# Where a layer input's projection lies: behind the end of the first projection, or beside the cached attention

## The chip, the cores and the metric

One NeuronCore of a Trainium2 chip runs the whole program. It has TensorE (PE: matrix products and transposes, with its weight loads shown apart as PEld), VectorE (DVE), ScalarE (ACT), GpSimd (POOL), and SyncE (SP), whose queue issues all of this kernel's transfers in order. The metric is the device time of one execution in microseconds (us); lower is better.

## The reference

One layer of a streaming encoder, over a prompt of 1024 tokens and 8 decode rows of 16 tokens with a cached past of 1024 (DEPTH is 1, D_MODEL 1024). Cut to what matters here:

```python
h = rmsnorm(x, g_mix)
q_a, k_a, v_a, q_b, k_b, v_b = split_heads(h, w_in)      # two groups of 8 heads x 64
a = stick_breaking(q_a, k_a, v_a, q_pos, k_pos)          # group A: sigmoid, running product over keys
o_b = chunk_band_prompt(q_b, k_b, v_b, rel_table)        # group B: softmax over 9 chunks of 64, with a bias
mix = jnp.concatenate([rmsnorm(a), rmsnorm(o_b)], axis=-1)
x = x + mix @ w_out
h = rmsnorm(x, g_ffn)
x = x + (silu(h @ w_gate) * (h @ w_up)) @ w_down
gate = sigmoid(rmsnorm(x, g_ple) @ w_ple_gate)
x = x + gate * (p @ w_ple_proj)                          # p: the layer input, 256 wide
```

The last line's `p @ w_ple_proj` depends on nothing else: it may be computed at any time, is stored to HBM, and is read again at the kernel's end. It is the work that the change moves.

## The kernel before

All products are of float32 accuracy: an operand is split in a high part (a cast on ScalarE, `whi`, `hTh`, `wth`, `pTh`) and the rest (a subtraction, `wlo`, `hTl`, `wtl`, `pTl`), and three products are summed (`mm3`, lines 100 to 102). Weights pass through the class `Chunks`: `raw` loads one chunk (`wraw`, one buffer), `parts` splits it into one of two places (`pair`), casting on ScalarE (line 159) and subtracting on GpSimd (line 105). So a third chunk can be split only when the products of the first have been read, and a new chunk loaded only when the last one is split.

The work is written as generators, and a few helpers interleave them: `advance(main, side, ratio, steps)` takes steps of `main` and `ratio` steps of `side` after each, and `along(a, b, ratio, due)` makes one sequence of two. Their numbers set the order in which work is handed to a scheduler, which then orders each engine's queue by its own estimate of when operands are ready. The engines run their queues strictly in that order.

In order of time:
- `qkv`: the first projection, in chunks of `w_in`, the last of them being queries of group B; first beside the cached attention of group A, then beside the prompt's attention, 1.95 units of it per step. It ends near 510 us.
- `attention`: 128 units, one for a head and a tile of 128 queries; eight units make a head, the first eight heads are group A. A unit's scores go to a bank `S` (two banks), for group A through two sigmoids on ScalarE (`w` and `keep`, lines 582 and 583), a running product on VectorE (`between`: `TENSOR_TENSOR_SCAN`, lines 111 and 114) and a product on GpSimd (line 592). Five units later `flip` transposes the weights (line 610) and splits them (`wth`, `wtl`); `outputs` multiplies with the values (`po`, lines 633 and 634), `turn` transposes a head's result (`ob`, line 648). In group B there is a bias and a minimum on VectorE (line 586) and an exponential on ScalarE (line 594). Sigmoid and exponential need different tables: at a switch ScalarE has an `ACT_TABLE_LOAD`.
- behind the projection: the cached attention of group B (`decode(1, ...)`: transposes of the cache `draw`, scores `sdec`, results `acc`) and `embed`, the layer input's projection, beside 43 units of attention. `embed` asks for its weights at its first step; SP issues that transfer far ahead, in the projection, but their split comes behind the product on GpSimd of the last group-A unit (`tc.issue_after(kept[-1].ins)`). Then, for each of nine token tiles, `turned` loads the layer input (`pn`, line 833), transposes and splits it (`pT`), and two steps of six products each (`pj`) follow, in the same banks `S`; ScalarE copies them out (`pjo`, line 853).
- `half_out`, beside the rest of attention: `mix` fetches finished heads (`mixn`, lines 894 and 898), transposes them (line 904) and casts them (`hUh`, line 907); then products with the first half of `w_out` (`acc`). Where attention has ended, the other heads' `mixn` follow, and the second half (`lower`, line 1001).
- the feed-forward part, the gate and the final norm, from some 820 us on.

Of the kernel before, what the change touches and what calls it, by code (L numbers as in the profile page):

```python
# [17 lines left out]
ALU = mybir.AluOpType  # L18
# [4 lines left out]
P = 128  # L23
D = 1024
# [15 lines left out]
def tile_hymba_step(  # L40
# [38 lines left out]
    V, A, G, T = nc.vector, nc.scalar, nc.gpsimd, nc.tensor  # L79
# [19 lines left out]
    def mm3(out, ah, al, bh, bl, start, stop):  # L99
        T.matmul(out, lhsT=ah, rhs=bh, start=start, stop=False)  # L100
        T.matmul(out, lhsT=ah, rhs=bl, start=False, stop=False)  # L101
        T.matmul(out, lhsT=al, rhs=bh, start=False, stop=stop)  # L102

    def sub(eng, out, a, hi):
        return eng.tensor_tensor(out, a, hi.bitcast(F32), op=ALU.subtract)  # L105

    def between(keep, own):

        n, d = keep.shape[1], own.shape[1]
        rev = keep[:, n - d :][:, ::-1]  # L110
        V.tensor_tensor_scan(rev, rev, own[:, ::-1], 0.0, op0=ALU.mult, op1=ALU.max)
        if n > d:
            rev = keep[:, : n - d][:, ::-1]
            V.tensor_tensor_scan(rev, rev, zero[:, 0:1].to_broadcast([P, n - d]), keep[:, n - d : n - d + 1], op0=ALU.mult,  # L114
                                 op1=ALU.max)
# [50 lines left out]
    def cols(w, c, n=256):  # L166
        return w[:, c * n : (c + 1) * n].rearrange("(k p) c -> p k c", p=P)
# [59 lines left out]
    def qkv(ch, hT, stg, first, second):  # L227
# [75 lines left out]
        def load(i, cuts=2):  # L303
            if i < len(loads):
                grp, w, c = loads[i]
                ready[loads[i]] = ch.load(cols(w_in[0], (grp * 3 + w) * 2 + c), KT, 256, cuts)

        ready[loads[0]] = first
        for i, (grp, w, c) in enumerate(loads):
# [200 lines left out]
            yield  # L510


    kept = []

    def attention(ap_, ps, lag):
        def prepare(p8):
# [30 lines left out]
        def bias(st, hh):  # L547
            if st["pr"] or hh:
                toep = ap_.tile([P, (8 - hh * 2) * P], F32, name="toep", tag=f"keep{1 + hh}")[:, :640]
            else:  # L550

                toep = ps["early"].tile([P, 640], F32, name="toep", tag="toep", bufs=1)
            nc.sync.dma_start(toep, rel[st["pr"] * 2 + hh])
            if st["pr"] or hh:
                G.tensor_scalar(toep, toep, -1.0, None, op0=ALU.mult)
            else:
                A.activation(toep, toep, AF.Copy, scale=-1.0)
            G.memset(toep[0:64, 576:640], -NEG)
            G.memset(toep[64:128, 0:64], -NEG)
            st[hh]["toep"] = toep  # L560

        def scores(st, hh, t):
            grp, hd = st["grp"], st[hh]
            if grp and "toep" not in hd:
                bias(st, hh)
            kb0 = max(0, t - 4) if grp else 0
            n = (t + 1 - kb0) * P
            w = ap_.tile([P, (t + 1) * P], F32, name="w", tag=f"wa{t}")[:, :n]
            if not grp:
                keep = ap_.tile([P, (7, 8, 6)[t % 3] * P], F32, name="keep", tag=f"keep{t % 3}")[:, :n]  # L570
            cut = {5: 384, 6: 512, 7: 512, 8: 512}.get(n // P, n)
            qs = slice(t * P, (t + 1) * P)
            mx = None
            for lo, hi in ((0, cut), (cut, n)):
                if lo == hi:
                    break
                sc = ps["s"].tile([P, 512], F32, name="S", tag="S")[:, : hi - lo]
                kc = slice(kb0 * P + lo, kb0 * P + hi)
                T.matmul(sc, lhsT=hd["qq"][:, qs], rhs=hd["kkh"][:, kc], start=True, stop=False)  # L579
                T.matmul(sc, lhsT=hd["qq"][:, qs], rhs=hd["kkl"][:, kc], start=False, stop=True)  # L580
                if not grp:
                    A.activation(w[:, lo:hi], sc, AF.Sigmoid)
                    A.activation(keep[:, lo:hi], sc, AF.Sigmoid, scale=-1.0)  # L583
                else:
                    m = ap_.tile([P, 1], F32, name="mxp", tag="mxp", bufs=6)
                    V.tensor_tensor_reduce(w[:, lo:hi], sc, hd["toep"][:, 640 - n + lo : 640 - n + hi], 1.0,
                                           3e38 if mx is None else mx, ALU.add, ALU.min, accum_out=m)
                    mx = m
            if not grp:
                between(keep, ident)  # L590
                G.memset(w[:, n - 1 :], 0.0)
                kept.append(G.tensor_tensor(w[:, : n - 1], w[:, : n - 1], keep[:, 1:], op=ALU.mult))  # L592
            else:
                A.activation(w, w, AF.Exp, bias=mx, scale=-1.0, accum_out=st["rs"][:, hh, t : t + 1])
            return w
# [125 lines left out]
    def pool(stack, name, side, bufs=1):  # L721
        return stack.enter_context(tc.tile_pool(name=name, bufs=bufs, side=side, reuse_waits="tile"))
# [10 lines left out]
    def advance(main, side, ratio, steps=None):  # L733

        due, n = 0.0, 0
        while steps is None or n < steps:
            if next(main, "end") == "end":
                break
            n += 1
            due += ratio  # L740
            while due >= 1.0:
                due -= 1.0
                next(side, None)
        return n

    ch = Chunks(pool(ctx, "w1", "left"), "w", 2048, 1, 2)
# [10 lines left out]
    with tc.tile_pool(name="x1", bufs=2, side="right") as xp, tc.manual_schedule(engines=all_engines):  # L757
# [26 lines left out]
        transposed(ps["t"], rows.pop(0), hT, 0)  # L784
        rows += [row(1), row(2)]
        project = qkv(ch, hT, stg, w_first, ch.raw(cols(w_in[0], 3), KT, 256))
        next(project)
        transposed(ps["t"], rows.pop(0), hT, 1)
# [16 lines left out]
    dec = decode(0, Chunks(dp, "d", 1024, RAWS, 2), dp)  # L805
# [11 lines left out]
    att = run(range(8))  # L817
# [6 lines left out]
    dec = decode(1, Chunks(dp, "d", 1024, RAWS - 1, 2), dp)  # L824
    pp = ps["early"] = pool(dstack, "pp", "right", 2)

    def embed():

        with tc.issue_after(kept[-1].ins):
            wj = ch.load(w_ple_proj[0].rearrange("(k p) c -> p k c", p=P), 2, D)  # L830
        def turned(t):
            pn = pp.tile([P, 256], F32, name="pn", tag="pn")
            nc.sync.dma_start(pn, p_tok[t])
            pt = ps["t"].tile([P, 512], F32, name="pt", tag="T")
            for j in range(2):
                T.transpose(pt[:, j * P : (j + 1) * P], pn[:, j * P : (j + 1) * P], ident)
            pT = [pp.tile([P, 2, P], F32R, name=f"pT{n}", tag=f"pT{n}", bufs=PT) for n in "hl"]
            pv = pt[:, :256].rearrange("p (k n) -> p k n", k=2)
            A.copy(pT[0], pv)
            sub(V, pT[1], pv, pT[0])  # L840
            return pT

        nxt = turned(0)
        yield
        for t in range(NT):
            pT = nxt
            for c in range(2):
                cs = slice(c * 512, c * 512 + 512)
                ps_ = ps["s"].tile([P, 512], F32, name="pj", tag="S")
                for k in range(2):  # L850
                    mm3(ps_, pT[0][:, k], pT[1][:, k], wj[0][:, k, cs], wj[1][:, k, cs], k == 0, k == 1)
                o = pp.tile([P, 512], F32, name="pjo", tag="pjo", bufs=2)
                A.copy(o, ps_)
                nc.sync.dma_start(proj[t * P : (t + 1) * P, cs], o)
                if c == 0 and t + 1 < NT:
                    nxt = turned(t + 1)
                yield
# [5 lines left out]
    def along(a, b, ratio, due):  # L863

        for _ in a:
            yield
            due += ratio
            while due >= 1.0:
                due -= 1.0
                if next(b, "end") != "end":  # L870
                    yield
        yield from b

    next(dec)
    advance(att, dec, 0, 3)
    beside = along(dec, embed(), 1.2, -3.0)
    advance(att, beside, 1.0, 40)
    for _ in beside:
        pass
    dstack.close()  # L880
# [85 lines left out]
    def bank(n=512):  # L966
        return ps_o.tile([P, 512], F32, name="ps", tag="O")[:, :n]
# [15 lines left out]
    def gate_up_parts(v, eng=None):  # L983
        return ch.parts(v, KT, 256, 4, eng)
# [101 lines left out]
    def sum_parts(i, v, eng=G):  # L1086
        out = [p4.tile([P, 4, P], F32R, name=f"S{i}{n}", tag=f"S{i}{n}", bufs=1) for n in "hl"]
        marks[:] = A.copy(out[0], v[i]), sub(eng, out[1], v[i], out[0])
        return out
# [7 lines left out]
    with ExitStack() as planned:  # L1097
        for i in range(NT + SKEW):
# [14 lines left out]
            if j == NT - 2:  # L1113
                w = gate_up_parts(raw, V)
# [15 lines left out]
    with tc.tile_pool(name="ph4b", bufs=2, side="right", reuse_waits="tile") as p4b:  # L1130
# [12 lines left out]
        for i in range(n_chunk):  # L1143
# [25 lines left out]
            c = bank()  # L1169
# [37 lines left out]
            if more:  # L1207
                S, w = {**S_next, 3: sum_parts(3, s)}, nxt
# [401 lines left out]
    for p in range(4):  # L1610
# [14 lines left out]
        c = bank()  # L1625
# [90 lines left out]
```

## Time and profile before

| | us |
|---|---|
| median of 3 runs | 1716.88 |
| lowest and highest | 1714.91, 1718.3 |
| the profiled execution | 1712.64 |
| its span, in which the rows below lie | 1710.6 |
| mean granted TensorE clock in the span | 0.99 |

A row of a timeline gives start, length, engine, line, operation, what it writes and reads, and in brackets how long its engine stood idle before it and what ended that. A row of the chain of waits gives start, length and what. In a table by stretch each engine has its busy time and the number of its instructions; PEclk is the share of full clock that TensorE was granted. Matmuls are pipelined: the start of the next says more of one's cost than its own length.

### The profile page before, as it was taken

The page shows a single profiled execution, that of the slowest core. Times are in us where ns is not written, and L with a number is a line of the kernel's source. Part 1 is how long each engine was busy: PE and PEld are TensorE (multiplying, and loading weights), DVE is VectorE, ACT ScalarE, POOL GpSimd, SP SyncE. Part 2 cuts the span into 40 slices and gives each one's busy share as a digit, 9 for nine tenths or more (in the row PEclk, how much of TensorE's full clock was granted, in tenths as well). Part 3 has the DMA queues.
Part 4 walks back from the last instruction along what each step waited for, and adds up shares of the span by engine and source line. Part 5 has one row for each costly group of instructions (what it writes and reads, how often), then busy time and mean ns, then how long its engine had stood idle before and what let it go on. Part 6 is the DMA issues. An engine that isn't in the chain of part 4 may idle for free.

```text
span 1710.6 us, 27738 instructions
## 1 busy us (share of the span) xinstructions
PE 1651.7 (97%) x10308; PEld 1421.3 (83%) x10308; DVE 1099.0 (64%) x1716; ACT 807.1 (47%) x1713; POOL 805.7 (47%) x652
## 2 busy tenths in 40 slices
PE   8999999989997999898989999999999999999998
PEld 7999888989996887787868888888888878878887
DVE  6111444379889666854787666666565597798875
ACT  5323545366778777643543233333332244433673
POOL 2313301277356411322345555555555379968763
PEclk9999999999998999999999999999999999999999
DMA  5847888665369885854422222222222597722222
GB/s 193 276 151 219 275 292 293 187 187 168 116 181 277 276 266 163 252 176 169 153 82 96 96 96 95 96 93 87 86 89 95 214 367 256 257 79 111 99 98 99
DMA packets 172810, 293.49 MB, mean 172 GB/s; under 512 B 16642, under 2 KB 96258, under 8 KB 170371
## 3 DMA queue, kind: packets, MB, share of 16 engines
q1 hardware_dynamic: 172674, 291.71, 52.0%
q8 instruction: 82, 1.34, 0.3%
q14 instruction: 54, 0.43, 0.1%
HBM read 204.77 MB, written 86.90 MB: 171 GB/s over the span
## 4 chain that ended last, share of the span: by engine, by line
PE 78%; DVE 7%; DMA 6%; ACT 3%; POOL 3%; issue 2%; SPq 1%; POOLq 0%; DVEq 0%; ACTq 0%
PE ps L1058 24%; PE ps L100 6%; PE ps L101 6%; PE ps L102 6%; PE pt L1321 4%; PE pt L1058 3%; PE ps L1321 3%; PE pt L610 2%; PE pt L405 2%; PE acc L468 2%; DMA v<-sv 2%; DVE keep L114 2%; PE po L634 1%; PE sdec L427 1%; PE S L579 1%
## 5 line engine op out<-in xcount | busy, mean ns | idle before, releaser
L105 POOL TENSOR_TENSOR wlo<-wraw,whi 128x512 fp32r<-128x512 f32 (+1 forms) x119 | 211.3, 1798 | 139.7 <-ACT whi L159 138.5
L100 PE MATMUL ps<-whi,hTh 128*128 128x256 f32 x576 | 167.7, 291 | 1.3 <-ACT st L267 1.3
L101 PE MATMUL ps<-wlo,hTh 128*128 128x256 f32 x576 | 164.2, 285 | 0.0
L102 PE MATMUL ps<-whi,hTl 128*128 128x256 f32 x576 | 163.7, 284 | 0.1
L159 ACT CAST whi<-wraw 128x512 fp32r<-128x512 f32 (+1 forms) x122 | 88.6, 744 | 71.4 <-PE ps L1058 28.6
L100 PEld LDWEIGHTS ps<-whi,hTh 128*128 128x128 f32 x576 | 110.4, 192 | 7.9 <-issue 5.7
L592 POOL TENSOR_TENSOR w<-w,keep 128x127 f32<-128x127 f32 (+4 forms) x64 | 78.6, 1230 | 74.8 <-DVE keep L114 64.5
L102 PEld LDWEIGHTS ps<-whi,hTl 128*128 128x128 f32 x576 | 110.4, 192 | 0.8 <-DVE hTl L105 0.4
L101 PEld LDWEIGHTS ps<-wlo,hTh 128*128 128x128 f32 x576 | 110.5, 192 | 0.2
L614 ACT CAST wth<-pt 128x512 fp32r<-128x512 f32 (+1 forms) x192 | 84.4, 466 | 44.5 <-PE pt L610 43.9
L105 DVE TENSOR_TENSOR wtl<-pt,wth 128x512 fp32r<-128x512 f32 (+1 forms) x192 | 94.1, 513 | 14.8 <-ACT wth L614 14.7
L114 DVE TENSOR_TENSOR_SCAN keep<-keep,zero 128x128 f32<-128x128 f32 (+7 forms) x64 | 101.6, 1588 | 1.7
L610 PE MATMUL pt<-ident,w 128*128 128x128 f32 x528 | 90.4, 284 | 8.5 <-DVE wtl L105 4.4
L610 PEld LDWEIGHTS pt<-ident,w 128*128 128x128 f32 x528 | 64.2, 144 | 21.6 <-DVE wtl L105 6.0
L579 PE MATMUL S<-qk 128*128 128x384 f32 (+2 forms) x192 | 71.9, 376 | 6.5 <-ACT keep L583 4.4
L633 PE MATMUL po<-wth,vk 128*128 128x256 f32 (+1 forms) x304 | 76.5, 283 | 1.5 <-DVE wtl L105 1.2
L105 POOL TENSOR_TENSOR actl<-actr,acth 128x1024 fp32r<-128x1024 f32 (+1 forms) x22 | 61.2, 2782 | 34.2 <-DMA sr<-acts 20.7
L634 PE MATMUL po<-wtl,vk 128*128 128x256 f32 (+1 forms) x304 | 73.4, 285 | 0.0
L406 DVE COPY kT<-pt 128x512 f32<-128x512 f32 x48 | 33.0, 687 | 53.4 <-PE pt L405 49.5
L101 PE MATMUL ps<-hTl,whi 128*128 128x384 f32 x192 | 65.4, 341 | 0.0
L102 PE MATMUL ps<-hTh,wlo 128*128 128x384 f32 x192 | 65.3, 340 | 0.0
L100 PE MATMUL ps<-hTh,whi 128*128 128x384 f32 x192 | 65.3, 340 | 0.0
(441 smaller groups left out, 5292.1 us busy)
## 6 DMA issues: line engine op xcount, KB each, us to landing
draw<-in_cache_sb_k SPq DMA_DIRECT2D x32, 512.0 KB, 5.7
draw<-in_cache_sb_v SPq DMA_DIRECT2D x32, 512.0 KB, 5.7
act<-sg SPq DMA_DIRECT2D x11, 1152.0 KB
actr<-act SPq DMA_DIRECT2D x22, 576.0 KB, 9.5
wraw<-in_w_in SPq DMA_DIRECT2D x11, 1024.0 KB, 8.7
wraw<-in_w_gate SPq DMA_DIRECT2D x11, 1024.0 KB, 5.5
wraw<-in_w_up SPq DMA_DIRECT2D x11, 1024.0 KB, 5.4
v<-sv SPq DMA_DIRECT2D x36, 256.0 KB, 4.7
```

The costliest lines, as they stand in the source:

```text
L100: T.matmul(out, lhsT=ah, rhs=bh, start=start, stop=False)
L101: T.matmul(out, lhsT=ah, rhs=bl, start=False, stop=False)
L102: T.matmul(out, lhsT=al, rhs=bh, start=False, stop=stop)
L105: return eng.tensor_tensor(out, a, hi.bitcast(F32), op=ALU.subtract)
L114: V.tensor_tensor_scan(rev, rev, zero[:, 0:1].to_broadcast([P, n - d]), keep[:, n - d : n - d + 1], op0=ALU.mult, op1=ALU.max)
L159: A.copy(h[:, o], v[:, o])
L579: T.matmul(sc, lhsT=hd["qq"][:, qs], rhs=hd["kkh"][:, kc], start=True, stop=False)
L610: T.transpose(pt[:, (c - c0) * P : (c - c0 + 1) * P], w[:, c * P : (c + 1) * P], ident)
L614: A.copy(wth[:, ks, qs], pv)
L634: T.matmul(dst, lhsT=vs, rhs=wtl[:, kb - base, c0:c1], start=False, stop=(i == nkb - 1))
L1058: T.matmul(out, lhsT=a[x][:, k], rhs=b[y][:, k], start=(not more and k == 0 and n == 0), stop=(k == 3 and n == 2), skip_group_check=more)
L1321: T.matmul(out, lhsT=a[i][:, x, m * P : (m + 1) * P], rhs=b[j][:, x], start=(not more and x == 0 and n == 0), stop=(x == 1 and n == 2), sk ...
```

## The change

The weights of `embed` are loaded and split inside `qkv`, at the beginning of its last chunk, where that loop has no further chunk to load. Their transfer keeps its place in SP's queue; what moves is the split, and with it the one load buffer comes free earlier for the first output weights. `embed` begins before the cached attention of group B: its first tile is transposed at once, and six of its steps go beside the three attention units that before had only the cache's first transfers. The rest follows at 0.65 steps per step of the cached attention, from the first on, where before it was 1.2, beginning behind about three. And both together lie beside 34 attention units and not 40, so that `half_out` begins six units earlier.

```diff
--- before.py
+++ after.py
@@ -304,6 +304,8 @@
             if i < len(loads):
                 grp, w, c = loads[i]
                 ready[loads[i]] = ch.load(cols(w_in[0], (grp * 3 + w) * 2 + c), KT, 256, cuts)
+            else:
+                late.append(ch.load(w_ple_proj[0].rearrange("(k p) c -> p k c", p=P), 2, D))
 
         ready[loads[0]] = first
         for i, (grp, w, c) in enumerate(loads):
@@ -510,7 +512,7 @@
             yield
 
 
-    kept = []
+    late = []
 
     def attention(ap_, ps, lag):
         def prepare(p8):
@@ -589,7 +591,7 @@
             if not grp:
                 between(keep, ident)
                 G.memset(w[:, n - 1 :], 0.0)
-                kept.append(G.tensor_tensor(w[:, : n - 1], w[:, : n - 1], keep[:, 1:], op=ALU.mult))
+                G.tensor_tensor(w[:, : n - 1], w[:, : n - 1], keep[:, 1:], op=ALU.mult)
             else:
                 A.activation(w, w, AF.Exp, bias=mx, scale=-1.0, accum_out=st["rs"][:, hh, t : t + 1])
             return w
@@ -826,8 +828,8 @@
 
     def embed():
 
-        with tc.issue_after(kept[-1].ins):
-            wj = ch.load(w_ple_proj[0].rearrange("(k p) c -> p k c", p=P), 2, D)
+        wj = late[0]
+
         def turned(t):
             pn = pp.tile([P, 256], F32, name="pn", tag="pn")
             nc.sync.dma_start(pn, p_tok[t])
@@ -871,10 +873,12 @@
                     yield
         yield from b
 
+    proj_units = embed()
+    next(proj_units)
     next(dec)
-    advance(att, dec, 0, 3)
-    beside = along(dec, embed(), 1.2, -3.0)
-    advance(att, beside, 1.0, 40)
+    advance(att, proj_units, 2.0, 3)
+    beside = along(dec, proj_units, 0.65, 0.0)
+    advance(att, beside, 1.0, 34)
     for _ in beside:
         pass
     dstack.close()
```

On TensorE, just behind the projection, before: flips of group A (`w`), then scores of 384 and 512 columns, then flips again.

```order
L633 MATMUL po<-wth,vk 128x128
L634 MATMUL po<-wtl,vk 128x128
L610 MATMUL pt<-ident,w 128x128 x7
L579 MATMUL S<-qk 128x384
L580 MATMUL S<-qk 128x384
L579 MATMUL S<-qk 128x512
L580 MATMUL S<-qk 128x512
L610 MATMUL pt<-ident,w 128x128 x8
```

Now, from the scores of 384 columns on (the row ahead of them is the scores of 256): the layer input's transposes stand in front of the flips and outputs.

```order
L581 MATMUL S<-qk 128x384
L582 MATMUL S<-qk 128x384
L838 MATMUL pt<-ident,pn 128x128 x2
L612 MATMUL pt<-ident,w 128x128 x6
L635 MATMUL po<-wth,vk 128x256
L636 MATMUL po<-wtl,vk 128x256
```

Behind the outputs that follow, products of the layer input:

```order
L635 MATMUL po<-wth,vk 128x128
L636 MATMUL po<-wtl,vk 128x128
L100 MATMUL pj<-whi,pTh 128x512
L101 MATMUL pj<-wlo,pTh 128x512
L100 MATMUL pj<-whi,pTh 128x512
L101 MATMUL pj<-wlo,pTh 128x512
L102 MATMUL pj<-whi,pTl 128x512
L100 MATMUL pj<-whi,pTh 128x512
L101 MATMUL pj<-wlo,pTh 128x512
L102 MATMUL pj<-whi,pTl 128x512
L838 MATMUL pt<-ident,pn 128x128 x2
L102 MATMUL pj<-whi,pTl 128x512
```

So the flips and outputs that stood ahead of the scores of 384 columns now stand behind them and behind the transposes of `pn`, and six steps of products lie among the flips of the last group-A head. Before, the first `pj` stood behind the first scores of group B.

On SP's queue at the same place (`sq`, `sk` and `sv` are what the cached attention reads, `vk` the values and `qk` the queries and keys of a head, `toep` a bias table), before:

```order
L365 DMA sk_6736<-kT1h 128x4x128
L370 DMA sv<-v_79 128x2x512
L141 DMA draw<-in_cache_cb_k 128x2x512
L553 DMA toep<-in_rel_table 128x640
L833 DMA pn<-in_p_prompt 128x256 x2
L531 DMA qk<-qT1h 64x1024
L531 DMA qk<-qT1l 64x1024
L531 DMA qk<-kT1h 64x1024 x2
```

Now:

```order
L141 DMA draw<-in_cache_cb_k 128x2x512
L543 DMA vk<-v_78 128x8x128
L367 DMA sq_6746<-qT1h 128x4x128
L141 DMA wraw<-in_w_out 128x4x512
L835 DMA pn<-in_p_prompt 128x256
L367 DMA sq_6748<-qT1l 128x4x128
L835 DMA pn<-in_p_prompt 128x256
L555 DMA toep<-in_rel_table 128x640
L533 DMA qk<-qT1h 64x1024
```

The second load of output weights (`wraw`) has come in ahead of the first `pn`, and `toep` and one of the `sq` have gone behind it. The first load of output weights stands some thirty rows further ahead, among the projection's last transfers.

On ScalarE, where attention ends (`any` is a one-column sigmoid that calls for its table), before, with all exponentials (`w,rsum`) done:

```order
L159 CAST whi<-wraw 128x1024
L637 COPY ob<-po 128x256
L159 CAST whi<-wraw 128x1024
L1093 ACT_TABLE_LOAD
L1093 ACTIVATE any<-nhalf 128x1
L637 COPY ob<-po 128x256
L907 ACTIVATE hUh_9125<-pt,g_out 128x384
L907 ACTIVATE hUh_9127<-pt,g_out 128x384
```

Now:

```order
L596 ACTIVATE w,rsum<-w,mxp 128x640
L159 CAST whi<-wraw 128x1024 x2
L1097 ACT_TABLE_LOAD
L1097 ACTIVATE any<-nhalf 128x1
L616 CAST wth<-pt 128x3x128
L616 CAST wth<-pt 128x4x128
L911 ACTIVATE hUh_8949<-pt,g_out 128x384
L911 ACTIVATE hUh_8951<-pt,g_out 128x384
L655 ACTIVATE ob<-osb 128x512
L596 ACT_TABLE_LOAD
L596 ACTIVATE w,rsum<-w,mxp 128x640
```

The casts of the second half's output weights and the sigmoid's table load have moved in front of the last unit's exponential, which needs its own table again. ScalarE has two table loads more: that one, and one at the first sigmoid of the feed-forward part.

## The prediction

> **What bounds the kernel now.** I read the page first, then busy time by stretch, then the timeline of the stretches in which TensorE falls short, and the chain of waits there. The page's line of busy time shows one engine as the bound:
>
> ```profile
> PE 1651.7 (97%) x10308; PEld 1421.3 (83%) x10308; DVE 1099.0 (64%) x1716; ACT 807.1 (47%) x1713; POOL 805.7 (47%) x652
> ```
>
> So the change can win only what TensorE loses: idle time, and busy time at half clock. Busy time by stretch (start and end, length, PE, PEld, DVE, ACT, POOL, granted clock, DMA share, GB/s):
>
> ```profile
> core 0: us, PE busy (x) PEld busy (x) DVE busy (x) ACT busy (x) POOL busy (x), PEclk, DMA share, GB/s
> 440.00:510.00 70.00, 70.00 (x481) 68.05 (x480) 61.11 (x91) 51.11 (x120) 31.91 (x46) 1.00 0.54 151
> 516.00:528.00 12.00, 7.71 (x38) 5.34 (x36) 11.96 (x14) 7.95 (x21) 8.05 (x7) 0.77 1.10 331
> 528.00:548.00 20.00, 18.39 (x136) 15.97 (x137) 18.85 (x32) 15.99 (x41) 13.91 (x20) 0.88 0.83 237
> 548.00:560.00 12.00, 8.70 (x66) 6.11 (x69) 9.64 (x17) 9.85 (x22) 6.80 (x7) 0.72 0.86 214
> 560.00:680.00 120.00, 118.01 (x1078) 96.28 (x1070) 80.83 (x260) 87.12 (x240) 32.21 (x42) 1.00 0.77 238
> 680.00:720.00 40.00, 33.27 (x230) 30.27 (x229) 32.48 (x92) 30.96 (x79) 14.08 (x12) 0.91 0.93 262
> 720.00:790.00 70.00, 70.00 (x396) 60.34 (x395) 36.63 (x95) 26.12 (x64) 12.07 (x9) 1.00 0.50 169
> 790.00:812.00 22.00, 17.04 (x98) 13.40 (x96) 8.62 (x17) 10.05 (x17) 9.92 (x6) 0.92 0.60 203
> ```
>
> The projection runs to about 510 with PE full. Lost time is idle plus busy times (1 - clock). 516 to 528: 4.3 + 1.8 = 6.1 us. 528 to 548: 1.6 + 2.2 = 3.8. 548 to 560: 3.3 + 2.4 = 5.7. 680 to 720: 6.7 + 3.0 = 9.7. 790 to 812: 5.0 + 1.4 = 6.3. From 560 to 680, where the layer input's products lie now, PE is busy 98%, and from 720 to 790 wholly: a product taken out of there shortens the kernel, one put in lengthens it. From 516 to 528 VectorE is the bound (11.96 of 12), and PE stands for it:
>
> ```profile
> 522.11 0.39 PE L633 MATMUL po<-wth,vk 128*128 128x256 f32 x1 [1.19 <-DVE wtl L105]
> 523.53 1.07 PE L610 MATMUL pt<-ident,w 128*128 128x128 f32 x4
> 526.31 0.90 PE L610 MATMUL pt<-ident,w 128*128 128x128 f32 x3 [1.71 <-DVE wtl L105]
> 526.87 0.67 PE L579 MATMUL S<-qk 128*128 128x384 f32 x1
> 530.57 0.38 ACT L583 ACTIVATE keep<-S 128x256 f32<-128x256 f32 x1
> 520.75 0.90 SPq L833 DMA_DIRECT2D pn<-in_p_prompt  x2
> DMA to landing us min/median/max: 8.9/8.9/8.9
> ```
>
> **The change, part by part.** *Products into the stretch behind the projection.* Their price:
>
> ```profile
> L100 PE MATMUL pj<-whi,pTh x36: 387/397/499, 567.3 to 679.2; 128*128 128x512 f32 x36
> 718.26 0.39 PE L102 MATMUL acc<-whi,hUl 128*128 128x512 f32 x1
> 718.49 0.40 PE L100 MATMUL acc<-whi,hUh 128*128 128x512 f32 x1
> 560.80 0.60 PE L610 MATMUL pt<-ident,w 128*128 128x128 f32 x4
> 561.15 0.36 PE L579 MATMUL S<-qk 128*128 128x256 f32 x1
> ```
>
> Products of this width start 0.23 us apart (718.26 to 718.49); four transposes and the step to the next work take 0.35 (560.80 to 561.15), so one is put at 0.11, a little over a quarter of it. 108 of them (3 x 36) run from 567 to 679. In the new order 42 stand ahead of the first score of the second head group, with five pairs of token transposes: 42 x 0.23 + 10 x 0.11 = 10.8 us, from a full stretch into one that loses time.
>
> They cannot start before the first pair of `pn` transposes, which stands right behind the scores of 384 columns. Those scores need ScalarE, which before reached the `keep` of 256 columns at 530.57; `pn` was issued at 520.75 and took 8.9 us, to 529.6 (one landing measured, the median line above). So the fill begins near 530, and the 6.1 us of 516 to 528 stay. A little is added there: the outputs and flips that ran at 522.11 and 523.53 now stand behind the transposes. They are 1.4 and 1.1 us of work; VectorE has scans to go on with, so I take 1.0, between 0 and 2.5.
>
> From 528 on 9.5 us (3.8 + 5.7) are lost. What stays of it? The restart at half clock, 2.2 (row 528 to 548). And ScalarE's table loads, which keep their place in front of the last group-A sigmoids:
>
> ```profile
> 548.04 1.28 ACT L450 ACT_TABLE_LOAD   x1
> 549.34 0.73 ACT L450 ACTIVATE wdec<-wdec,mx 128x528 f32<-128x528 f32 x1
> 550.18 1.28 ACT L582 ACT_TABLE_LOAD   x1
> ```
>
> Two of 1.28 with the exponential between them hold up every score bank, and PE's scores of that place stand ahead of more products: 2.6 stay. So 9.5 - 2.2 - 2.6 = 4.7 come back. Bounds: all 9.5, or nothing. The term: -4.7 + 1.0 = -3.7 us.
>
> *Splits.* The weights of this projection are split ahead of 510, and the first load of output weights, which takes the place of the projection's last, is split just behind its end:
>
> ```profile
> L105 POOL TENSOR_TENSOR wlo<-wraw,whi 128x1024 fp32r<-128x1024 f32 x4 | 9.4, 2376 | 2.0 <-ACT whi L159 2.0
> 523.14 0.41 DVE L111 TENSOR_TENSOR_SCAN keep<-keep,ident 128x128 f32<-128x128 f32 x1
> 526.50 2.03 DVE L111 TENSOR_TENSOR_SCAN keep<-keep,ident 128x128 f32<-128x128 f32 x1
> ```
>
> Each is two subtractions of 2.38 us on GpSimd and two casts on ScalarE. Near 455 GpSimd has 38 of 70 us free and ScalarE 19: hidden, the cover being their own idle time. The output weights' split now lies at about 505 to 516, just ahead of VectorE's full stretch; the two rows show one scan at 0.41 and at 2.03 us with GpSimd at work beside it. At most 2 x 1.6 = 3.2, at least 0; I take 0.8, nearer to nothing since VectorE is not yet full there.
>
> *Attention units.* Six units leave the stretch before 680 for that of the half output projection: PE-bound there, 98% busy here, so 0. The time lost at 680 to 720 hangs on transfers:
>
> ```profile
> 692.79 8.88 DMA wraw<-in_w_out
> 701.74 7.07 DMA mixn<-mixp
> ```
>
> The third load of output weights still waits for the split that follows the last product of the layer input, and mixes still stand behind it in SP's queue: 0, between -3 and +3.
>
> *The end of attention.* Before, PE waited for late `mixn` transfers, and its products reached to the last unit:
>
> ```profile
> 799.15 6.82 DMA mixn<-mixp
> 806.11 1.51 PE L904 MATMUL pt<-ident,mixn 128*128 128x128 f32 x6 [3.87 <-DMA mixn<-mixp]
> 795.26 0.44 PE L648 MATMUL pt<-ident,ob 128*128 128x128 f32 x2 [0.24 <-ACT ob L637]
> 802.13 2.04 POOL L671 TENSOR_TENSOR osb<-osb,r_o 128x512 f32<-128x512 f32 x2
> 766.26 0.83 ACT L594 ACTIVATE w<-w,mxp 128x640 f32<-128x640 f32 x1 [0.22 <-DVE mxp L586]
> 789.60 1.05 ACT L159 CAST whi<-wraw 128x1024 fp32r<-128x1024 f32 x1 [0.75 <-PE acc L102]
> 793.46 1.28 ACT L1093 ACT_TABLE_LOAD   x1
> ```
>
> With six more units beside the side work, the earlier mixes are fetched and turned in time. What then remains is the chain from the last `ob` transposes to the normed `osb`, 795.26 to 804.17, 8.9 us, with 27 products (6.2 us) and nine transposes (1.0) behind which PE can hide: 1.7 lost, 2.5 with some half clock, instead of 6.3: -3.8. Against that, all products of the half output projection now end ahead of the last scores. Between them and the last unit's flip PE has 37 transposes and 12 products of outputs, 5.5 us. ScalarE has in that place two weight casts (2.1), a table load each way (2.6), four smaller casts and a square (about 3) and the exponential (0.8): 8.5 to 9.5. Where it bounds, up to 4.0 are lost; if it is ahead, none; I take 2.0. Also one load more stands at the first sigmoid of the feed-forward part: +0.6, between 0 and 1.28.
>
> As the Trainium skill has it (ScalarE: Activation LUTs, What ACT_TABLE_LOAD costs), a switch costs about 1.28 us and a drain of 1.38, 2.66 together. The trace shows the 1.28 but no drain: the exponential starts at 549.34, as the load ends. By the page the two loads at the end and the one of the feed-forward part would take 1.38 more each, some 3.5 with half of the last one hidden, and the sum would be near -0.6.
>
> **The sum.** -3.7 + 0.8 + 0 - 3.8 + 2.0 + 0.6 = -4.1 us. The profiled execution took 1712.64 us (span 1710.6), 4.2 below the median of 1716.88. It would become 1708.5, and the median 1712.8.
>
> **Rivals.** *Fed throughout.* If `pn` lands by 526, the restart and the loads' share come back too, another 4.8: 1708.0. For it: the work is ready and needs no VectorE but a short subtraction. Against: PE's queue is in order, and the products share two banks with scores that ScalarE must empty. The clock was full wherever PE was busy throughout (1.00 from 440 to 510) and fell where it stood (0.77). The Trainium skill has the same rule (TensorE: Matmul & The Clock Gate, HAM oscillation): no idle gaps over some 3.4 us keep the full rate, by which a filled PE would win this case's 4.8.
>
> *Nothing gained.* The products only change places: each holds up the group-A units behind it by its own 0.23 us, and PE in the new place is no better fed than before (it is busy 18.39 of 20 from 528 to 548 already). Then the first term is about 0 and the end of attention pays for itself: 1717. Here it would also end if table loads cost more than their rows: were ScalarE idle once more for each load's length, the three would take 3.2 us more (the last one half hidden), 1716.0. The rows at 548 to 551 show no such idling, so it has 0.03 of this case's chance.
>
> *Slower.* The `pn` transfers now stand in SP's queue behind the second load of output weights, 1 MB, which may not be issued before GpSimd has ended the first half's split. PE's transposes stand ahead of the flips, so each us that `pn` lands behind 530 starves VectorE's scans and costs about one. That load is 1024 KB where 320 KB of `toep` and 256 KB of `sq` stood: at 331 GB/s 1.4 us; held up by a whole load (8.88), it is 1712.8 + 8.9 = 1721.7. It decides from about 4 us, a landing behind 534.
>
> **How the numbers follow.** Forecast, -2 to -8, 0.33 (own range 1709 to 1715); fed throughout 0.13; nothing gained 0.30; slower 0.24. A difference under 0.2% (3.4 us) can't be told from none. The part of the forecast under that bound and the part of the third case beyond it are taken as equal: faster 0.46, same 0.30, slower 0.24. The range reaches from halfway below the first rival, 1704, to the slower case, 1722.
>
> **What would show it.** In the profile after: the first `pj` products at 528 to 533; PE at full clock and busy over 90% from 536 to 560; no wait of PE for `pn` past 531; first split of `w_out` near 510 with scans beside it under 1 us; the last `pj` near 665 to 672; the wait for `mixn` behind the last `ob` gone, and two table loads around the last exponential. I am wrong if PE stands for `pn` for over 4 us, if PE's losses from 516 to the last score of group A exceed 15 us, or if the end of attention loses more than 7.

## The result: slower, by 5 to 8 us

The changed kernel took 1722.94 us (median of 7 runs, 1721.51 to 1728.66) beside 1715.68 of the kernel before (7 runs): a ratio of 1.0047, 95% interval 1.0032 to 1.0062. Timed once more it was 1.0028 (1.0017 to 1.0039). The forecast was 1712.8, with a range of 1704 to 1722. The profiled execution took 1722.94 us, its span is 1720.9.

The page's line of busy time, and the stretches that the prediction showed, with one more from unit 48 to unit 64 (start and end, length, PE, PEld, DVE, ACT, POOL, granted clock, DMA share, GB/s), now of the changed kernel:

```profile
PE 1656.9 (96%) x10308; PEld 1423.8 (83%) x10308; DVE 1099.5 (64%) x1716; ACT 808.3 (47%) x1715; POOL 806.3 (47%) x652
440.00:510.00 70.00, 69.88 (x476) 67.73 (x474) 63.83 (x88) 50.39 (x121) 36.91 (x47) 1.00 0.59 162
502.40:572.00 69.60, 57.88 (x352) 49.12 (x351) 55.95 (x79) 49.34 (x118) 35.66 (x47) 0.88 0.85 251
516.00:528.00 12.00, 8.41 (x53) 7.09 (x51) 11.93 (x14) 8.28 (x19) 6.58 (x8) 0.86 1.03 326
528.00:548.00 20.00, 15.81 (x75) 12.98 (x76) 13.62 (x20) 10.77 (x29) 14.46 (x19) 0.74 0.84 254
548.00:560.00 12.00, 12.00 (x91) 10.59 (x90) 6.39 (x14) 8.02 (x21) 2.25 (x4) 1.00 0.68 198
560.00:680.00 120.00, 117.14 (x1073) 90.90 (x1072) 81.30 (x250) 87.98 (x234) 29.67 (x44) 0.99 0.75 226
680.00:720.00 40.00, 32.34 (x219) 28.14 (x219) 31.50 (x99) 28.76 (x77) 11.12 (x10) 0.96 0.92 243
720.00:790.00 70.00, 67.08 (x383) 58.07 (x382) 35.76 (x97) 27.12 (x70) 16.95 (x15) 1.00 0.61 188
790.00:812.00 22.00, 19.42 (x132) 17.53 (x132) 13.65 (x32) 15.56 (x33) 4.72 (x2) 0.92 0.66 216
```

TensorE is full from 548 to 560, as foretold, but the 20 us before lose 4.2 idle and half of much of the rest (clock 0.74, where it was 0.88), and VectorE, which the last scans of group A bounded, now stands for a third of them (13.62 of 20, where it was 18.85). Fixed stretches hold other work in each kernel, so the same instruction is better followed. Starts in us after the first score of unit 48 (498.88 before, 502.38 and 501.76 in the changed kernel's two profiles); the last two columns are kernels told of below:

| instruction on TensorE | before | changed | changed, again | load later | split held |
|---|---|---|---|---|---|
| first `pj` | 68.4 | 33.7 | 33.7 | 30.0 | 29.0 |
| score of unit 59 | 29.9 | 40.5 | 40.3 | 35.7 | 33.2 |
| score of unit 64 (first of group B) | 57.0 | 69.7 | 69.5 | 66.3 | 64.2 |
| score of unit 72 | 90.1 | 106.0 | 105.8 | 98.3 | 98.5 |
| first product of the half output | 218.8 | 211.7 | 211.6 | 204.0 | 202.0 |
| its last product | 293.1 | 292.9 | 292.1 | 288.0 | 282.5 |
| first product of the feed-forward part | 296.9 | 311.4 | 310.7 | 305.3 | 299.8 |
| first `ps<-B11h` | 370.5 | 378.4 | 377.6 | 372.3 | 368.2 |
| end of the span | 1211.7 | 1218.6 | 1218.4 | 1211.5 | 1210.2 |

The two profiles of the changed kernel agree within 1.0 us in each row. Ahead of unit 48 all kernels run the same rows, and differ by chance (last section). The table's 6.7 to 6.9 us lie between the two timings, 4.8 and 8.1.

Where unit 59 loses its 10.5 us, in the changed kernel's timeline, engine by engine:

```profile
516.39 3.17 DVE L114 TENSOR_TENSOR_SCAN keep<-keep,zero 128x512 f32<-128x512 f32 x1
522.05 0.86 SPq L141 DMA_DIRECT2D wraw<-in_w_out  x1
522.95 2.57 SPq L835 DMA_DIRECT2D pn<-in_p_prompt  x1
531.49 0.66 PE L838 MATMUL pt<-ident,pn 128*128 128x128 f32 x2 [1.49 <-DMA pn<-in_p_prompt]
535.40 0.38 ACT L585 ACTIVATE keep<-S 128x256 f32<-128x256 f32 x1 [4.48 <-POOL w L594]
535.68 0.37 ACT L841 CAST pTh<-pt 128x256 fp32r<-128x256 f32 x1
535.82 1.24 DVE L111 TENSOR_TENSOR_SCAN keep<-keep,ident 128x128 f32<-128x128 f32 x1 [2.24 <-ACT keep L585]
536.10 0.50 PE L100 MATMUL pj<-whi,pTh 128*128 128x512 f32 x1 [1.11 <-ACT pTh L841]
542.61 0.43 DVE L105 TENSOR_TENSOR pTl<-pt,pTh 128x256 fp32r<-128x256 f32 x1 [3.20 <-ACT pTh L841]
542.83 0.48 PE L581 MATMUL S<-qk 128*128 128x512 f32 x1
```

TensorE waits 1.49 us for `pn`, no more; from there to unit 59's score it waits 3.85 us in all (1.49, 1.11, and 1.25 for `pTl` at 538.54), and part of its work runs at half clock. ScalarE stands 4.48 us for a buffer of `keep` that a product on GpSimd has to free, and the cast `pTh` of the layer input stands behind that sigmoid in its queue, with nothing to wait for but its turn (its transposes began at 531.49). The first products come at 536.10, and the score of unit 59 stands behind 12 of them at 542.83. Then VectorE has no scan to do: it idles 2.24 and 3.20 us in the place where it was the bound.

At attention's end the prediction's order came as told: the wait for `mixn` behind the last `ob` is gone, all half-output products end ahead of the last unit, and the table is loaded twice round its exponential:

```profile
744.71 0.33 PE L612 MATMUL pt<-ident,w 128*128 128x128 f32 x1 [2.92 <-DVE wtl L105]
795.26 0.39 PE L102 MATMUL acc<-whi,hUl 128*128 128x512 f32 x1
796.76 1.28 ACT L1097 ACT_TABLE_LOAD   x1
800.60 1.28 ACT L596 ACT_TABLE_LOAD   x1
801.89 0.83 ACT L596 ACTIVATE w<-w,mxp 128x640 f32<-128x640 f32 x1
804.06 0.33 PE L612 MATMUL pt<-ident,w 128*128 128x128 f32 x1 [1.60 <-DVE wtl L105]
813.82 0.48 PE L100 MATMUL ps<-whi,hUh 128*128 128x512 f32 x1
```

From the last product of the half output to the first of the feed-forward part it is 18.6 us, where it was 3.8: attention is late, and nothing is left to lie beside it. 744.71 is a new wait inside the half output.

### The profile page after: what moved, and what is told of

Same layout as the page of the kernel before. It is cut to its first block, busy times and chain, and to the rows that moved or that the text cites. A ratio compares the mean times of both kernels' runs of the same rounds, so it can differ in the third digit from the quotient of the medians.

```text
span 1720.9 us, 27734 instructions
## 1 busy us (share of the span) xinstructions
PE 1656.9 (96%) x10308; PEld 1423.8 (83%) x10308; DVE 1099.5 (64%) x1716; ACT 808.3 (47%) x1715; POOL 806.3 (47%) x652
## 4 chain that ended last, share of the span: by engine, by line
PE 79%; DMA 6%; DVE 6%; ACT 4%; POOL 3%; issue 2%; SPq 1%; POOLq 0%; DVEq 0%; ACTq 0%
PE ps L1062 24%; PE ps L100 6%; PE ps L102 6%; PE ps L101 6%; PE pt L1325 5%; PE ps L1325 4%; PE pt L1062 3%; PE pt L407 2%; PE pt L612 2%; PE acc L470 2%; DMA v<-sv 2%; PE sdec L429 2%; PE po L636 1%; PE po L635 1%; DMA mixn<-mixp 1%
## 5 line engine op out<-in xcount | busy, mean ns | idle before, releaser
L114 DVE TENSOR_TENSOR_SCAN keep<-keep,zero 128x128 f32<-128x128 f32 (+7 forms) x64 | 107.7, 1685 | 1.7
L105 DVE TENSOR_TENSOR wtl<-pt,wth 128x512 fp32r<-128x512 f32 (+1 forms) x192 | 94.4, 512 | 13.5 <-ACT wth L616 13.3
```

## The experiments

Ratios are of each kernel to the kernel before timed beside it on the same chip, with 95% intervals; 0.1% is 1.7 us.

| kernel | ratio | interval |
|---|---|---|
| changed; again | 1.0047; 1.0028 | 1.0032 to 1.0062; 1.0017 to 1.0039 |
| split_only | 1.0019 | 1.0008 to 1.0030 |
| before34 | 1.0000 | 0.9988 to 1.0012 |
| pace_only | 0.9991 | 0.9982 to 1.0001 |
| no_six; again | 0.9982; 0.9999 | 0.9974 to 0.9991; 0.9985 to 1.0012 |
| no_six40 | 0.9995 | 0.9984 to 1.0007 |
| units40 | 1.0014 | 1.0003 to 1.0024 |
| three | 1.0037 | 1.0022 to 1.0052 |
| spread | 1.0005 | 0.9996 to 1.0013 |
| six_later | 0.9993 | 0.9984 to 1.0002 |
| after_drop | 0.9991 | 0.9978 to 1.0005 |
| no_six_drop | 0.9996 | 0.9983 to 1.0010 |
| after_hold; again | 0.9987; 0.9982 | 0.9976 to 0.9998; 0.9970 to 0.9994 |
| no_six_hold | 1.0055 | 1.0036 to 1.0074 |
| six_later_hold | 0.9994 | 0.9983 to 1.0006 |
| load_later | 0.9983 | 0.9972 to 0.9995 |

The repeat of the changed kernel, 1.0028, lies below the 1.004 to 1.006 expected of it, and that of no_six, 0.9999, above its 0.997 to 0.999: between two sets of runs of one kernel lies up to 0.2%.

### The parts one by one

The early split alone, in the kernel before (split_only):

```diff
+            else:
+                late.append(ch.load(w_ple_proj..., 2, D))
...
-        with tc.issue_after(kept[-1].ins):
-            wj = ch.load(w_ple_proj..., 2, D)
+        wj = late[0]
```

> The early load and split of the weights alone; the order of the work and the 40 units as before. Theory S (the output weights' split now lies at 510 to 518 us, and VectorE's scans beside its two subtractions take 1.5 and 3.2 us where they took 0.4 and 1.3): slower by 3 to 4 us, 1719 to 1720. Theory T (the loss is all at attention's end, where fewer units lie beside the side work): as before, 1715 to 1717. Theory M (the six early steps hold up group A): as before too.

34 units alone (before34), 0.65 alone (pace_only), and the changed kernel without its early steps (no_six):

```diff
-    advance(att, beside, 1.0, 40)
+    advance(att, beside, 1.0, 34)          # before34
...
-    beside = along(dec, embed(), 1.2, -3.0)
+    beside = along(dec, embed(), 0.65, 0.0)     # pace_only
...
-    next(proj_units)
-    advance(att, proj_units, 2.0, 3)
+    advance(att, dec, 0, 3)                # no_six
```

> The kernel before with 34 attention units beside the cached attention and not 40, and nothing else. Theory T: side work ends ahead of the last scores, attention's last units stand alone, with two table loads more; what the trace of the changed kernel has lost from the first half output product to the feed-forward part, 3.4 + 1.1 = 4.5 us, comes by this alone: 1719 to 1721. Theories S and M: the earlier mixes save the wait of 3.9 us for the transfer at 802: 1712 to 1716.

> The kernel before, with 0.65 steps of the layer input's projection per step of the cached attention from the first on, and nothing else (late split, 40 units, no early steps). The split alone took 1.0019 and the split with this pace 0.9995: theory A (the two add): 0.996 to 0.998 of before, 1709 to 1713. Theory I (the pace only gives back what the early split costs): 0.999 to 1.001.

> The changed kernel without the six early steps and transposes: early split, 0.65 steps from the first on, 34 units. Theories S and T together: both costs stay, 1715.7 + 3.8 + 4.5 = 1724, as the changed kernel or a little above. Theory M: the loss goes, 1716 to 1718.

> The kernel without the early steps once more, beside the held one on the same chip; every theory: 0.997 to 0.999 of before.

The split costs 3.3 us by itself (1.0019). 0.65 alone takes 0.9991, in the range of theory I. 34 units cost nothing, though attention's end looks there as in the changed kernel: 17.3 us instead of 3.8 between half output and feed-forward part, which 3.2 us less in the half output's products, 5.2 less in the feed-forward part and 3.9 less ahead of both give back. So theory T fell as a cause by itself. Without the early steps the loss is gone (0.9982 and 0.9999): it comes with the six steps, and theory M stood, with the split's cost not seen in that combination.

The number of units, with and without the early steps (40 for 34):

> The changed kernel with 40 units beside the cached attention and not 34; no other number differs, and the two table loads at attention's end are gone. Theory T: the end's share is given back, and the split's stays: 1718 to 1720. Theory M (the six steps cost by themselves): 1722 to 1724, no better. Theory S alone says nothing of it: 1722 to 1724.

> The kernel without the early steps (early split, 0.65 steps from the first on), with 40 units in place of 34. Theory U (the number of units matters only where attention is late already, as with the six steps): 1714 to 1716, as with 34. Theory V (the gain of that kernel is the earlier start of the half output projection): the gain goes, 1718 to 1720, as with the split alone.

No difference without the steps. With them 40 units took 1.0014, better than the changed kernel's two values, but the two profiles, from unit 48 on, are equal (1218.9 and 1218.6 us), and that of units40 is of its slowest run (1723.15, median 1719.39): inconclusive.

### The price of a product in either place

In the first three tiles one product is computed for each half, not six; 30 of 108 are left out, everything else stays.

```diff
+                if t < 3:
+                    T.matmul(ps_, lhsT=pT[0][:, 0], rhs=wj[0][:, 0, cs], start=True, stop=True)
+                else:
                     for k in range(2): mm3(...)
```

> The changed kernel, in which the first six steps have one product each and not six (left out: 30 of 108 products of the layer input, 6.9 us of TensorE at 0.23 each); transposes, transfers and copies stay. Theory B: their full price is on the path, 1725.5 less 7 to 9: 1716 to 1719. Theory F (they do fill gaps, and the loss is elsewhere: transfer, tables, order of SP's queue): 1722 to 1726.

> The same 30 products left out of the kernel without the early steps, where they lie beside the cached attention at 560 to 600 us. If TensorE bounds that stretch, as the 98% busy of the page had it: 1714.6 less 6.9, 1707 to 1709. If another engine bounds it (a matmul's modelled end hides waits): less than half of that, 1711 to 1715. Theory B says that the price there is lower than in the block.

In the new place the 30 products are worth 0.37 to 0.56% (1.0028 or 1.0047 to 0.9991), 6.4 to 9.6 us: their price of 6.9, or more. In the old place nothing can be measured: 0.9996 against 0.9982 and 0.9999, worse than both theories had it. Yet from unit 48 to unit 92 they are worth 5.1 us there too, with every other TensorE instruction of that stretch the same (first no_six, then the kernel with 30 products fewer):

```profile
500.45:660.34 159.89, 147.45 (x1306) 120.32 (x1305) 125.51 (x307) 118.88 (x315) 62.18 (x85) 0.98 0.83 245
499.78:654.54 154.76, 142.01 (x1276) 115.14 (x1276) 125.14 (x307) 117.99 (x315) 62.16 (x85) 0.98 0.84 252
```

Between the same units they are worth 6.5 us in the new place (175.1 and 168.6 us). Of the 5.1 us, 4.3 are lost again by unit 96. The timeline shows where (the kernel with the products left out; the last row is the same place in no_six):

```profile
657.47 0.41 PE L838 MATMUL pt<-ident,pn 128*128 128x128 f32 x2 [2.42 <-DMA pn<-in_p_sample]
655.35 21.48 SPq L859 DMA_DIRECT2D proj<-pjo  x8
677.07 0.47 SPq L533 DMA_DIRECT2D qk<-qT1h  x1
664.22 14.08 SPq L856 DMA_DIRECT2D proj<-pjo  x7
```

TensorE then stands 2.42 us for the last `pn`, with a window of half clock behind it (the following products take 0.63 and not 0.39). In this kernel that transfer stands behind the next head's queries and keys in SP's queue (issued at 650.84), in no_six ahead of them (649.34). SP then stands over eight stores of `pjo` for 21.48 us (in no_six over seven for 14.08), and the queries behind them are issued 177.3 us after unit 48, in no_six 178.1. So the products had their price in the old place, and waits for transfers took the time back, one of them in an order of SP's queue that the scheduler had made anew. What the time alone shows is not the price.

### Where the block stands

Three steps and not six (three); one step beside each of six units (spread); the six beside the next three units (six_later):

```diff
-    advance(att, proj_units, 2.0, 3)
+    advance(att, proj_units, 1.0, 3)                                   # three
+    advance(att, proj_units, 1.0, 6)                    # spread, 31 units behind
+    advance(att, dec, 0, 3); advance(att, proj_units, 2.0, 3)   # six_later, 31 units behind
```

> The changed kernel with three of the early steps and not six (18 products and two or three pairs of transposes ahead of the last group-A units). On a scale where the kernel before takes 1717.7, the changed one takes 1725.5 and the one without the early steps 1714.6. Theory B (the products stand as one block in PE's queue ahead of the scores that VectorE's scans wait for, and cost what they take): half of the 11 us, 1719 to 1721. Theory L (what costs is that the first transposes wait for the layer input's transfer, ahead of flips and outputs, one step or six): 1723 to 1725.

> The changed kernel with the six early steps one beside each of six attention units, not two beside each of three (and 31 units behind). Theory B: the scores come between the products, half of the loss returns, 1.000 to 1.003 of before. Theory G: 1.004 to 1.006. Theory L (the first transposes' wait for the layer input): 1.004 too, since the first pair stands where it stood.

> The changed kernel with the block of six early steps three attention units further back (three units alone first, as before; then six steps beside three units; then the rest, 31 units). Theory B (the block costs because group A's last scores, which VectorE's scans wait for, stand behind it in PE's queue): behind more of group A the block does less harm, 1.000 to 1.003 of before. Theory G (any products beyond what the cached attention leaves free there put attention off, wherever they stand): 1.004 to 1.006, as the changed kernel.

> The changed kernel once more, on the chip of the next three, so that the steps can be set side by side. Every theory: 1.004 to 1.006 of the kernel before.

Six steps elsewhere, or spread, cost nothing that can be measured (0.9993, 1.0005), three in the first place nearly all (1.0037). So it is not the number of products put there (theory G fell), and theory B's price by the product's length does not hold for three either: three lies in theory L's range alone, and spread, which L would have as slow, in theory B's. In three and in spread ScalarE stands 4.3 to 4.5 us ahead of `pTh` as above; the two differ in that the cached attention starts three units later in spread; what that gives was not tried by itself. So the blocked cast alone does not make the loss: spread has it and loses nothing.

### Split or queue

The split of the first output weights held behind group A's last product on GpSimd (after_hold and, on the other kernels, no_six_hold and six_later_hold):

```diff
+            if c == 0:
+                raw = ch.raw(w_out[0, 0:512, 0:512]..., 4, 512)
+                with tc.issue_after(kept[-1].ins):
+                    wh, wl = ch.parts(raw, 4, 512, 2)
```

> The changed kernel with the split of the first output weights held back until the last product of group A on GpSimd (their transfer stays early). The second load of output weights then follows the first transfers of the layer input in SP's queue. Theory S (the split beside the scans costs some 3 us, and is a share of the loss): the scans at 511 to 518 take 0.4 and 1.3 us again, eight units end 3 us earlier, and 1.001 to 1.003 of before. Theory R (group A's last units are late by the block anyway, and the 3 us vanish in it): 1.003 to 1.005 as the changed kernel.

> The changed kernel with the held split once more, on the same chip: 0.998 to 1.000 by both theories.

> The same hold in the kernel without the early steps. Theory S: 0.996 to 0.997 of before, 1710 to 1712. Theory R': the split returns behind group A, where before it stood in the way of other work (559 to 564 us): 0.998 to 1.000, nothing gained.

> The same hold in the kernel whose six steps stand three units later. Theory S: 0.996 to 0.998 of before. Theory R': 0.999 to 1.000, as without it.

The loss is gone (0.9987, 0.9982), which neither theory had (1.001 at best), and eight units end 3.3 us earlier; the scan of 512 takes what it took before, 1.28 and not 3.17:

```profile
515.08 1.28 DVE L114 TENSOR_TENSOR_SCAN keep<-keep,zero 128x512 f32<-128x512 f32 x1
```

But the second load of output weights had moved, too. And in no_six the same hold costs 0.6 to 0.7% (1.0055), against both theories: its profile has 6.9 us more than no_six between units 92 and 104, where the last `pn` is late and the stores of `pjo` stand in SP's queue as in no_six_drop:

```profile
665.05 0.41 PE L839 MATMUL pt<-ident,pn 128*128 128x128 f32 x2 [2.52 <-DMA pn<-in_p_sample]
662.83 21.61 SPq L857 DMA_DIRECT2D proj<-pjo  x8
693.16 0.90 PE L907 MATMUL pt<-ident,mixn 128*128 128x128 f32 x3 [3.66 <-DMA mixn<-mixp]
```

So the last pair moves the second load alone, nine rows (11 transfers) back in SP's queue, behind the third `pn`; the split stays beside the scans:

```diff
-            nc.sync.dma_start(pn, p_tok[t])
+            firsts.append(nc.sync.dma_start(pn, p_tok[t]))
...
+            if c == 1:
+                with tc.issue_after(firsts[2].ins):
+                    raw = ch.raw(w_out[0, 0:512, 512:1024]..., 4, 512)
```

> The changed kernel with only the second load of output weights (1 MB) moved nine rows back in SP's queue, behind the first three transfers of the layer input and the heads' queries and keys. The split of the first output weights stays beside the scans. Held split and later load together took 0.9987 of before, the changed kernel 1.0028 and 1.0047. Theory S (the split beside the scans is the cost): 1.002 to 1.004, little gained. Theory Q (the load ahead of the layer input in SP's queue is the cost): 0.999 to 1.000.

0.9983: theory Q, a little under its range. The whole loss goes with one transfer's place and the orders that the scheduler makes from it, and the split is still there (unit 56 at 24.0 us after unit 48, as in the changed kernel, where the held split has 20.8). Its timeline at the place shown above:

```profile
522.27 1.04 SPq L836 DMA_DIRECT2D pn<-in_p_prompt  x1
532.51 0.38 SPq L141 DMA_DIRECT2D wraw<-in_w_out  x1
530.70 0.63 PE L839 MATMUL pt<-ident,pn 128*128 128x128 f32 x2
531.70 0.38 ACT L842 CAST pTh<-pt 128x256 fp32r<-128x256 f32 x1
536.33 0.38 ACT L586 ACTIVATE keep<-S 128x256 f32<-128x256 f32 x1 [3.25 <-POOL w L595]
533.26 0.45 PE L100 MATMUL pj<-whi,pTh 128*128 128x512 f32 x1
538.94 0.48 PE L582 MATMUL S<-qk 128*128 128x512 f32 x1
503.30:569.60 66.30, 55.70 (x368) 48.26 (x367) 54.52 (x82) 49.94 (x119) 37.53 (x50) 0.95 0.90 266
```

ScalarE still waits for GpSimd's buffer (3.25), but `pTh` now stands ahead of that sigmoid. The first products begin 3.7 us sooner after unit 48, unit 59's score 4.8, and in place of 0.88 the clock is 0.95 up to unit 64 (last row: from unit 48 to there). This kernel and the one with the held split beat the kernel before by 0.13 to 0.18%, 2 to 3 us; no_six did so once (0.9982) and not again (0.9999).

From unit 48 to unit 92 the changed kernel and this one run the same TensorE instructions, 1357 of them, in 175.1 and 168.1 us:

```profile
502.38:677.46 175.08, 163.36 (x1357) 131.29 (x1356) 125.07 (x309) 124.02 (x326) 61.60 (x85) 0.95 0.79 235
503.28:671.40 168.12, 157.19 (x1357) 128.57 (x1356) 123.59 (x309) 123.62 (x326) 62.51 (x85) 0.98 0.82 245
```

Of the 7.0 us, idle time gives 0.8 (11.7 and 10.9), and the clock, 0.95 and 0.98, some 5. Nor is that this profile alone: the mean granted clock of all timed runs is 0.988 and 0.989 in the two sets of the changed kernel and 0.988 in three, but 0.991 in spread, in load_later and in both sets of the held split. 0.003 of 1717 us is 5 us: most of what separates the first three from the others is half clock. The kernel before has 0.987 to 0.989 too. So against it the changed kernel loses by its block and not by the clock, and load_later seems to make up by the clock what its block still costs (unit 64 comes 9.3 us later than before).

What stays open: 3.4 of the 7 us are seen by unit 64, 7.7 by unit 72, in a stretch where TensorE's order differs in many places since the scheduler decided all that follows anew. Which of the waits there brings the half clock on was not told apart, and part of it is chance: no_six has 0.98 in one profile and 0.95 in the other, over the same instructions. Nor is it known why the scheduler put `pTh` on the other side of the sigmoid; that it reckoned with a later `pn` is only argued.

## Why the prediction was wrong, step by step

- **The first term, -4.7 + 1.0, failed: nothing was filled.** By the prediction's numbers the stretch from unit 48 to unit 64 had to grow by 10.8 put in, less 4.7 filled, plus 1.0 and 0.8: 7.9. It grew by 12.7. TensorE's idle time there was 9.2 us before (57.02 less 47.83) and is 11.7 now (69.60 less 57.88), at a clock of 0.89 and 0.88. Before:

```profile
498.88:555.90 57.02, 47.83 (x328) 41.29 (x328) 53.85 (x80) 45.12 (x109) 33.38 (x47) 0.89 0.91 263
```

The fill did not start at 530 but at 536, and not for `pn`'s landing (531.5) but for a cast behind a blocked sigmoid; of queues moved past, ScalarE's was the one not looked at. The 1.0 was for the flips and outputs behind the transposes. That the score of unit 59, from which VectorE's next scans start, comes behind 12 products and their waits, 10.5 us later, was in no term.
- **"A product taken out of there shortens the kernel" (560 to 680) held in place and failed in the time.** What follows unit 64 had to become 12.0 us shorter: 10.8 of products no longer there, and 1.2 at the end of attention. It became 5.8 shorter (12.7 late at unit 64, 6.9 at the end). The 30 products left out of the old place gave 5.1 of their 6.9 us by unit 92 and nothing measurable at the end, since waits for transfers stand behind them. The Trainium skill (Trainium Kernel Development and Optimization, Best Practices) judges how near a kernel is to its limit by MFU (the share of peak arithmetic) and the weight loads' share, not by the matmuls' busy time: PEld has 96.28 of 120 in that row, 80%, and 68.05 of 70 from 440 to 510. That only 74% of the price was seen agrees with it; no run prices a product in the fuller stretch.
- **Splits, +0.8.** 3.3 alone: the scans took 1.51 and 3.17 in place of 0.41 and 1.28, so it is the upper end (3.2). In the changed kernel it hardly counts: with it (load_later) and without (after_hold, hold_again) the time is the same within the intervals.
- **The end of attention, -3.8 + 2.0 + 0.6.** The order came as told, the wait for `mixn` went, and 34 units alone moved the time by 0.0 ± 0.12%, 1.2 less foretold: right within 2 us. That is luck in part: it is a balance of 13.5 us more between half output and feed-forward part and 12.3 less elsewhere, which the prediction did not have. With attention late by the early steps the same end is where the lateness is paid.
- **Half-output stretch.** Foretold as full before and after; the changed kernel has the 2.92 us at 744.71, which was in no term.
- **The slower rival** (held up by the second load, 1721.7, from a landing behind 534) named the right transfer and nearly the time, the latter by luck: its mechanism did not occur, since `pn` landed at 531.5, ahead of the point from which it was to decide. **Fed throughout** did not get its landing by 526, and fell with the clock of 0.74; **nothing gained** was right that each product holds up group A by its own time: with 10 of the 12 products ahead of it left out (after_drop), unit 59's score comes 2.2 us sooner.
- **Table loads**, 1.28 without a drain: 800.60 to the exponential at 801.89. The Trainium skill's 1.38 more (ScalarE: Activation LUTs, What ACT_TABLE_LOAD costs) is not seen here either.

## What to carry to other kernels

Before work is moved into idle time, leave some of it out in both places, and compare the two kernels up to a point where all else on the bound engine is the same, not by the time alone: here the price was 5.1 and 6.5 us of 6.9, so the move could win only by what it filled. Idle time in front of an engine that is waited for belongs to a chain; what is put into it must stand behind that chain's instructions in every in-order queue, the small casts and the transfers too. And when a scheduler orders the queues, one large load a few rows further ahead can change as much as all that was moved on purpose, 7 us here: read the order of each queue, not only of the bound engine's.

## What was not expected of the hardware

A scan of VectorE beside a subtraction on GpSimd took 3.17 us (from 516.39) where it takes 1.28 alone, same shape:

```profile
515.97 2.51 POOL L105 TENSOR_TENSOR wlo<-wraw,whi 128x1024 fp32r<-128x1024 f32 x1
```

From the subtraction's end, 518.48, the 1.28 would lead to 519.76; the scan ended at 519.56. The Trainium skill (SBUF — State Buffer, SBUF: two separate sides) has the two engines share a pair of ports as an exclusive lock, by which the scan, with two inputs in SBUF, waits until the other ends; the rows agree within 0.2 us.

Half clock comes in part by chance. These rows (one stretch ahead of everything that was changed; before, changed, three) have the same busy time and the same wait of 2.77 us in them:

```profile
160.00:190.00 30.00, 27.23 (x275) 23.72 (x274) 12.31 (x15) 13.84 (x36) 9.10 (x9) 1.00 0.79 237
160.00:190.00 30.00, 27.23 (x262) 23.15 (x261) 10.79 (x13) 13.48 (x36) 9.09 (x9) 0.94 0.73 223
160.00:190.00 30.00, 27.23 (x238) 23.72 (x237) 10.04 (x11) 12.31 (x32) 8.35 (x8) 0.89 0.73 222
```

A clock of 1.00, 0.94 and 0.89 over 30 us is none, some 3.6 and some 6.6 us at half rate. The profiled execution of before had no such stretch ahead of unit 48, which began at 498.9; in the other kernels' profiles it began at 499.0 to 504.4 and all had some. Single profiles are to be compared from the first differing instruction on, and one timed run decides nothing under 0.3% (35 runs of the kernel before on one chip lie from 1712.2 to 1720.9).
